# Start bytes of the tiles that TensorE reads, in a one-core hybrid decoder layer

## The chip, the core and the metric

The kernel runs on one core of one Trainium2 chip. The metric is the device time of one execution in microseconds (us). Three runs of the kernel before gave 320.55, 321.25 and 322.75 us, the median is 321.25 us. One further execution was profiled.

## What is computed

One pre-norm decoder layer over 256 tokens of width 1024, in float32, then a final RMSNorm:

```python
h = rms_norm(x, norm_g)
(qa, ka, va, ga, ub, vb, gb, qc, gc, ma, mb, mc) = split_cols(h @ w_in, IN_SPLITS)
out_a = moba_attention(rope(qa), rope(ka), va) * silu(ga)        # 6 heads of 128, causal
out_b = gmlp_spatial_gate(ub, vb, ln_g, w_spatial, b_spatial) * silu(gb)
out_c = memory_cross_attention(qc, rms_norm(mem, mem_norm_g), w_mem_kv) * silu(gc)
y = (sigmoid(ma) * (out_a @ w_branch_a) + sigmoid(mb) * (out_b @ w_branch_b)
     + sigmoid(mc) * (out_c @ w_branch_c))
x = rms_norm(x + y @ w_out, final_norm_g)
```

With 256 tokens there is one attention block, so branch A is plain causal attention. In branch B the spatial gate is `u * (tril(w_spatial) @ layer_norm(v) + b_spatial)`, with `b_spatial` added per token and group. Nearly all the work is the product of `h`, of the branch outputs and of `y` with weight matrices that are read once from HBM.

## The kernel before, in words

**Split operands.** Each float32 operand of the big products is cut into two parts of the type fp32r, a high and a low one. A product then takes three matmuls: high by high, high by low, low by high. The activations are cut once (`nh`/`nl`, `sh`/`sl`, `mh`/`ml`, `ah`/`al`, `obh`/`obl`, `och`/`ocl`, `yh`/`yl`). The weights are cut as they arrive: `split` (L250 to L270) lets ScalarE write `hi` (L260) and VectorE write `lo` as the weights minus `hi` (L264).

**Chunks.** The weights come in pieces of 128 partitions by 2048 floats. A piece is two chunks of 1024 columns each. `PLAN` and `chunks` (L189 to L202) give the order of all 136 chunks by hand. There are these kinds:

- `mvk` (L502, L508): keys and values of the memory tokens, the first eight chunks.
- `tok` (L481) and `fea` (L630): products of `n`. In `fea` the weights are the stationary operand, a chunk is eight matmuls of 512 columns with `hi` and eight of 256 columns with `lo`.
- `st` (L570): products of `n` and `s` with sums of weight blocks (a two by two scheme with seven products). Here `n` or `s` is stationary and `hi` or `lo` streams past it, six matmuls of 512 columns a chunk. The sums of weights are made by the DMA: a plain load into `form` (L233, SP queue), then an accumulating load on top of it (L236, GpSimd queue), and for some by VectorE (L240).
- `br` (L448 to L450 through `mm3`): the branch outputs `ah`/`al`, `obh`/`obl`, `och`/`ocl` are stationary, `hi` and `lo` stream. Twelve matmuls of 512 columns a chunk. Six `br` chunks take `ah` and `al`.
- `out` (the same lines): `y` with `w_out`, at the end; half of the second token tile in pieces of 256 columns.

**Buffers.** `hi` and `lo` are two tiles of five slots of 4096 bytes each (`SPL = 5`, L187). Chunk c uses slot c % 5, so it may be split when the matmuls of chunk c-5 have read that slot. `raw` has three buffers of 8192 bytes, `form0` and `form1` have 8192 bytes each.

**Order of the small work.** Attention, the spatial gate, softmax and the norms are units in a list. A planner, `Units` (L85 to L147), places them between the chunks by its own estimates of engine time and by due chunks. Loads are issued on the SP queue in program order, so a load waits behind the one ahead of it. `load` (L214) issues the pieces of plain weights, `load_wsp` (L698) the spatial weights with the spatial bias behind them in the same tile `wspb`, and `mix_gate` (L966) adds the bias to the mixed tokens and multiplies by `u`. Units decide the order of instructions while the program is built; nothing in it depends on run time.

**Where tiles begin.** Tiles are laid one behind another in each partition, in the order in which their tags first occur; a tile begins at a multiple of 32 bytes. In the built program before, the start bytes modulo 1024 are these:

| tile that TensorE reads | start byte modulo 1024 |
|---|---|
| `hi`, `lo` (weights, all five slots) | 736, 736 |
| `n`, `s`, `m`, `y` | 608 |
| `obh`, `obl`, `och`, `ocl` | 608 |
| `ah`, `al` | 736 |
| `cx`, `va`, `vb`, `wspb` | 608 |
| `qk` | 544 |

Inside a tile TensorE's operands begin at steps of 512 bytes (128 floats). So, modulo 512, the weights begin 128 bytes away from every activation except `ah` and `al`, which begin at the same byte. `raw` and `form0` begin at 736, `form1` at 608.

Of the kernel before, what the change touches and what calls it, by code (L numbers as in the profile page):

```python
# [24 lines left out]
F32 = mybir.dt.float32  # L25
# [3 lines left out]
OP = mybir.AluOpType  # L29
# [6 lines left out]
HA, GB, HC = 6, 6, 4  # L36
# [112 lines left out]


@with_exitstack
def tile_hybrid_layer(ctx: ExitStack, tc: tile.TileContext, mw, xT, mem, x, fin_g, ln_g, w, ws, w_sp, b_sp, rope, out):
    nc = tc.nc
    ctx.enter_context(tc.manual_schedule())
    const = ctx.enter_context(tc.tile_pool(name="const", bufs=1))
# [5 lines left out]
    V = {}  # L161

    def slot_tile(name, shape, tag, dt=F32):
        V[name] = act.tile(shape, dt, name=name, tag=tag)
        return V[name]
# [16 lines left out]
    def hsl(h):  # L182
        return slice(h * 128, (h + 1) * 128)


    LOPAD = 0
    RAW, SPL, LEAD, JT = 3, 5, 4, 2  # L187
    raw, hi, lo = {}, {}, {}
    chunks = []  # L189
# [17 lines left out]
    def raw_alloc(j):  # L207
        raw[j] = wts.tile([128, PIECE], F32, name="raw", tag="raw", bufs=RAW)

    def load_part(j, a, b):  # L210
        src = bass.AP(tensor=w.tensor, offset=w.offset + PLAIN.index(j) * 128 * PIECE + a, ap=[[PIECE, 128], [1, b - a]])
        nc.sync.dma_start(raw[j][:, a:b], src)

    def load(j):  # L214
        raw_alloc(j)
        parts = 2 if 18 <= j < 49 else 1
        for i in range(parts):
            load_part(j, i * PIECE // parts, (i + 1) * PIECE // parts)

# [30 lines left out]
    def split_alloc(c):  # L250
        if "hi" not in V:
            for n, pad in (("hi", 0), ("lo", LOPAD)):
                if pad:
# [442 lines left out]
        nc.sync.dma_start(V["lng"], rows(ln_g, BW))  # L696

    def load_wsp():  # L698
        t = slot_tile("wspb", [128, GB * 128 + 32], "trig")
        nc.sync.dma_start(t[:, 0:GB * 128 + GB], w_sp)  # L700
        V["wsp"], V["bst"] = t[:, 0:GB * 128].rearrange("p (g t) -> p g t", g=GB), t[:, GB * 128:GB * 128 + GB]

    def cut_wsp():
        for g in range(GB):
# [43 lines left out]
    U.add("consts", POOL, 1.3, setup_consts, after=["sx0"], wait=6.0)  # L748
    U.add("gmlp", None, 0, load_lng, after=["lns"], wait=8.0)
    U.add("wsp", None, 0, load_wsp, after=["rout2"], wait=8.0)  # L750
    U.add("cut", POOL, 1.6, cut_wsp, after=["wsp"])
    U.add("bsb", None, 0, load_bsb, after=["lna0", "lna1"], wait=8.0)
# [99 lines left out]
        return [] if n < 0 else [f"c{stage}{n}" if n < HC else f"a{stage}{n - HC}"]  # L852


    lst = const.tile([128, 2, 2], F32, name="lst")
    lrs = const.tile([128, 2], F32, name="lrs")

# [108 lines left out]
    def mix_gate(i, a):  # L966
        g = 2 * i + a
        pv, u = ST["mp", i][:, a * S:a * S + S].rearrange("p (t s) -> p t s", t=2), V["ut"][:, :, hsl(g)]
        nc.vector.scalar_tensor_tensor(u, pv, V["bst"][:, g:g + 1], u, op0=OP.add, op1=OP.mult)

    def turn_b(i):
        ST["bt", i] = p = bank()
# [48 lines left out]
    for i in range(2):  # L1021
        U.chain(f"mix{i}", (PE, 0.87, lambda i=i: mix_tok(i)), (DVE, 0.42, lambda i=i: mix_gate(i, 0)),
                (DVE, 0.42, lambda i=i: mix_gate(i, 1)), due=[at_br[0, 3] - 7 + i, at_br[0, 3] - 5 + i, at_br[0, 3] - 5 + i], after=["lna0", "lna1", "cut", "gts"])
# [125 lines left out]
    for c in range(n_br):  # L1149
        if chunks[c][0] == "st":  # L1150
            _, g, i, h = chunks[c]
# [6 lines left out]
    for c in range(n_br + 4):  # L1158
# [27 lines left out]
        if s % 2 == 1 and s // 2 in PLAIN:  # L1186
            q = PLAIN.index(s // 2) + 2
            if 4 < q < len(PLAIN):
                load(PLAIN[q])
            if q == 6:  # L1190
                load_mem()
# [132 lines left out]
```

## Time and profile before

| | value |
|---|---|
| runs | 320.55, 321.25, 322.75 us |
| profiled execution | 320.98 us |
| its span, from first to last instruction | 319.2 us |
| mean granted TensorE clock | 0.996 |
| matmuls | 1542 |
| first and last matmul, start | 0.84 us and 313.1 us |
| read from HBM | 73.02 MB |

The profile names an instruction by its line, its engine, its operation and its tiles, written `out<-in`. Matmuls overlap: a row's duration runs from the start of a matmul to its modelled end, so the time that a matmul takes from the stream is the distance between the start of it and the start of the next one. PEld is the loading of the stationary operand for the matmul to come, which runs while the one before streams. The chain of waits follows the last instruction back to what released it. In the windows view a number behind x counts the instructions that touch the window.

### The profile page before, as it was taken

How to read it: one execution, taken by the hardware profiler on the slowest of the kernel's cores; microseconds unless marked ns; L12 is line 12 of the kernel's file. 1: busy time of each engine (PE TensorE's matmuls, PEld its weight loads, DVE VectorE, ACT ScalarE, POOL GpSimd, SP SyncE). 2: the span in 40 equal slices, each digit the busy share in tenths (PEclk: the TensorE clock that was granted, in tenths of full speed). 3: DMA queues.
4: the chain of work that ended last, by engine and by line, in shares of the span. 5: the costliest groups of instructions: out<-in, count | busy, mean ns of one | idle time of the engine just before them, and what ended most of it. 6: DMA issues, size and time to landing. Idle time of an engine off the chain costs nothing.

```text
span 319.2 us, 4440 instructions
## 1 busy us (share of the span) xinstructions
PE 312.0 (98%) x1542; PEld 260.1 (81%) x1542; DVE 260.2 (81%) x376; ACT 227.8 (71%) x357; POOL 36.5 (11%) x55
## 2 busy tenths in 40 slices
PE   8999999999999999999999999999999999999992
PEld 4888888888888888888888888888888887888982
DVE  2878999996689887877599799998996599989432
ACT  3875989556997658877996968669758655576333
POOL 1000040030010013006003102004020031000022
PEclk9999999999999999999999999999999999999998
DMA  7999999789659879868967999778999789943003
GB/s 198 405 402 415 369 353 245 282 213 199 195 180 248 265 248 203 198 206 200 285 199 200 190 342 259 175 258 172 233 337 284 267 201 198 388 140 131 2 2 130
DMA packets 20470, 75.14 MB, mean 235 GB/s; under 512 B 2528, under 2 KB 3552, under 8 KB 18144
## 3 DMA queue, kind: packets, MB, share of 16 engines
q1 hardware_dynamic: 15984, 59.00, 52.3%
q0 software_dynamic: 4320, 15.73, 26.8%
q8 instruction: 12, 0.20, 0.2%
q10 hardware_dynamic: 144, 0.13, 0.1%
q14 instruction: 10, 0.08, 0.1%
HBM read 73.02 MB, written 1.05 MB: 232 GB/s over the span
## 4 chain that ended last, share of the span: by engine, by line
PE 77%; DMA 9%; DVE 6%; issue 4%; ACT 1%; POOL 0%; SPq 0%; ACTq 0%; POOLq 0%; DVEq 0%
PE acc L630 26%; PE acc L570 18%; DMA form<-in_ws_dram 7%; PE aux L502 3%; PE acc L508 3%; PE aux L570 3%; DVE lo L264 3%; PE acc L450 3%; PE acc L448 3%; PE acc L449 3%; PE aux L781 2%; DMA st<-in_mw_dram 2%; PE aux L481 2%; PE acc L481 2%; DVE form L240 1%
## 5 line engine op out<-in xcount | busy, mean ns | idle before, releaser
L264 DVE TENSOR_TENSOR lo<-form,hi 128x1024 fp32r<-128x1024 f32 x70 | 84.8, 1222 | 16.2 <-ACT hi L260 15.7
L260 ACT ACTIVATE hi<-form 128x1024 fp32r<-128x1024 f32 x70 | 73.4, 1057 | 23.3 <-DMA form<-in_ws_dram 8.6
L264 DVE TENSOR_TENSOR lo<-raw,hi 128x1024 fp32r<-128x1024 f32 x58 | 70.1, 1223 | 11.2 <-ACT hi L260 10.9
L260 ACT ACTIVATE hi<-raw 128x1024 fp32r<-128x1024 f32 x58 | 60.9, 1057 | 10.8 <-DMA raw<-in_w_dram 4.7
L630 PE MATMUL acc<-n,hi 128*128 128x512 f32 x240 | 61.0, 396 | 0.0
L236 POOL DMA_DIRECT2D form<-in_ws_dram x30 | 26.1, 871 | 232.9 <-DVE lo L264 84.6
L630 PEld LDWEIGHTS acc<-n,hi 128*128 128x128 f32 x240 | 43.9, 188 | 9.1
L570 PE MATMUL acc<-hi,s 128*128 128x512 f32 x96 | 33.1, 402 | 0.0
L630 PE MATMUL acc<-n,lo 128*128 128x256 f32 x240 | 32.5, 285 | 0.0
L630 PEld LDWEIGHTS acc<-n,lo 128*128 128x128 f32 x240 | 31.1, 188 | 1.5
L570 PE MATMUL acc<-hi,n 128*128 128x512 f32 x72 | 25.1, 404 | 0.0
L570 PEld LDWEIGHTS acc<-hi,s 128*128 128x128 f32 x96 | 18.1, 188 | 4.0
L570 PE MATMUL aux<-hi,s 128*128 128x512 f32 x64 | 21.1, 395 | 0.0
L570 PE MATMUL acc<-lo,s 128*128 128x512 f32 x48 | 18.9, 395 | 0.0
L570 PE MATMUL aux<-hi,n 128*128 128x512 f32 x48 | 16.1, 396 | 0.0
L570 PEld LDWEIGHTS acc<-hi,n 128*128 128x128 f32 x72 | 13.6, 188 | 2.9
L570 PEld LDWEIGHTS aux<-hi,s 128*128 128x128 f32 x64 | 12.1, 188 | 2.8
L570 PE MATMUL acc<-lo,n 128*128 128x512 f32 x36 | 14.2, 394 | 0.0
L570 PE MATMUL aux<-lo,s 128*128 128x512 f32 x32 | 12.7, 398 | 0.3 <-DVE lo L264 0.3
L643 ACT ACTIVATE qk<-acc 128x256 f32<-128x256 f32 x12 | 4.7, 390 | 11.7 <-PE acc L630 11.7
L240 DVE TENSOR_TENSOR form<-form,form 128x1024 f32<-128x1024 f32 x10 | 12.2, 1222 | 0.0
L570 PEld LDWEIGHTS aux<-hi,n 128*128 128x128 f32 x48 | 9.0, 188 | 2.1
(233 smaller groups left out, 581.8 us busy)
## 6 DMA issues: line engine op xcount, KB each, us to landing
raw<-in_w_dram SPq DMA_DIRECT2D x17, 1024.0 KB, 8.1
form<-in_ws_dram SPq DMA_DIRECT2D x30, 512.0 KB, 5.6
form<-in_ws_dram POOLq DMA_DIRECT2D x30, 512.0 KB, 8.5
raw<-in_w_dram SPq DMA_DIRECT2D x24, 512.0 KB, 7.3
st<-in_mw_dram SPq DMA_DIRECT2D x7, 384.0 KB, 7.5
raw<-in_w_dram SPq DMA_DIRECT2D x8, 256.0 KB, 7.2
xk<-in_x_dram SPq DMA_DIRECT2D x2, 512.0 KB, 7.5
xt<-in_xT_dram SPq DMA_DIRECT2D x2, 512.0 KB, 9.6
```

The source lines that it names most:

```text
L236: nc.gpsimd.dma_start(form_half(i, h), block(g, b, h), accum_op=OP.add)
L240: nc.vector.tensor_tensor(form_half(i, h), form_half(i, h), form_half(1 - i, h), OP.add)
L260: nc.scalar.activation(hi[c][:, a:b], raw[c // 2][:, o + a:o + b], AF.Copy)
L264: nc.vector.tensor_tensor(lo[c][:, a:b], raw[c // 2][:, o + a:o + b], hi[c][:, a:b].bitcast(F32), OP.subtract)
L448: nc.tensor.matmul(p, s_hi, m_hi, start=first, stop=False)
L449: nc.tensor.matmul(p, s_hi, m_lo, start=False, stop=False)
L450: nc.tensor.matmul(p, s_lo, m_hi, start=False, stop=last)
L481: nc.tensor.matmul(acc[name, o][t], src[:, k0 + i, tsl(t)], wt[c][:, i * 512:(i + 1) * 512], start=c == 8 and i + j == 0, stop=c == 11 and ...
L502: nc.tensor.matmul(acc["mv", 0][t][:, a:b], src[:, k, tsl(t)], wt[:, a:b], start=k + n == 0, stop=k == KD - 1 and n == len(parts) - 1)
L508: nc.tensor.matmul(p, wt, m, start=k == 0 and j < HC, stop=k == KD - 1 and j >= HC)
L570: nc.tensor.matmul(p, x[:, k0 + k, tsl(t)], wt[c][:, a * 512:(a + 1) * 512], start=first and a + j == 0, stop=half == 1 and a + j == 3, sk ...
L630: nc.tensor.matmul(o, wt, m, start=i == 0, stop=i == len(passes) - 1, skip_group_check=True)
```

## The change

Five edits:

1. The spatial bias gets a tile of its own, `b_col`, in the pool `const`. That pool grows by 32 bytes, and all tiles behind it move by that.
2. `wspb`, of 3200 bytes, becomes `wsp`, of 3072 bytes. Tiles behind it no longer stand 128 bytes further modulo 1024.
3. `LOPAD` goes from 0 to 64 floats: an unused tile of 256 bytes stands between `hi` and `lo`.
4. The spatial bias is loaded by a DMA of its own, 6 floats a partition, right behind that of the spatial weights on the SP queue. `mix_gate` takes it from `b_col`.
5. `load` cuts one piece of weights less into two DMAs (the bound 49 becomes 47).

Start bytes modulo 1024 in the built program, before and with the change:

| tile | before | with the change |
|---|---|---|
| `hi` | 736 | 640 |
| `lo` | 736 | 896 |
| `n`, `s`, `m`, `y`, `obh`, `obl`, `och`, `ocl` | 608 | 640 |
| `ah`, `al` | 736 | 640 |
| `cx`, `va`, `vb`, `wsp` | 608 | 640 |
| `qk` | 544 | 576 |
| `raw`, `form0`, `form1` | 736, 736, 608 | 640, 896, 640 |

```diff
-    LOPAD = 0
+    LOPAD = 64
...
-        parts = 2 if 18 <= j < 49 else 1
+        parts = 2 if 18 <= j < 47 else 1
...
     def load_wsp():
-        t = slot_tile("wspb", [128, GB * 128 + 32], "trig")
-        nc.sync.dma_start(t[:, 0:GB * 128 + GB], w_sp)
-        V["wsp"], V["bst"] = t[:, 0:GB * 128].rearrange("p (g t) -> p g t", g=GB), t[:, GB * 128:GB * 128 + GB]
+        slot_tile("wsp", [128, GB, 128], "trig")
+        nc.sync.dma_start(V["wsp"], w_sp)
+        nc.sync.dma_start(b_col, b_spt)
...
+    b_col = const.tile([128, GB], F32, name="b_col")
...
-        nc.vector.scalar_tensor_tensor(u, pv, V["bst"][:, g:g + 1], u, op0=OP.add, op1=OP.mult)
+        nc.vector.scalar_tensor_tensor(u, pv, b_col[:, g:g + 1], u, op0=OP.add, op1=OP.mult)
```

The host gives the bias as an array of its own, `b_spt`, no longer behind the spatial weights.

No engine's instructions change their order. Only the SP queue has other rows. Around the spatial weights it holds this before:

```order
L233 DMA form_401<-in_ws_dram 128x1024
L769 DMA qk<-mid 32x256 x4
L700 DMA wspb<-in_w_sp_dram 128x774
L233 DMA form_401<-in_ws_dram 128x1024
L212 DMA raw<-in_w_dram 128x1024 x2
```

and this with the change:

```order
L233 DMA form_403<-in_ws_dram 128x1024
L769 DMA qk<-mid 32x256 x4
L700 DMA wsp<-in_w_sp_dram 128x768
L701 DMA b_col<-in_b_spt_dram 128x6
L233 DMA form_403<-in_ws_dram 128x1024
L212 DMA raw<-in_w_dram 128x1024 x2
```

One small DMA stands ahead of the next `form` load. Further down, one piece of weights (that of the second `br` piece) comes as one DMA; here is the piece of the difference on the SP queue:

```order
 L212 DMA raw<-in_w_dram 128x1024 x2
-L233 DMA form_326<-in_ws_dram 128x1024 x2
-L212 DMA raw<-in_w_dram 128x1024 x2
-L233 DMA form_326<-in_ws_dram 128x1024 x2
+L233 DMA form_328<-in_ws_dram 128x1024 x2
+L212 DMA raw<-in_w_dram 128x2048
+L233 DMA form_328<-in_ws_dram 128x1024 x2
 L212 DMA raw<-in_w_dram 128x2048 x2
```

Two loads of 512 KB have become one of 1024 KB; the names of `form` differ only in a buffer number.

More of the change, by code (lines that the diff above doesn't have):

```diff
@@ L151, in tile_hybrid_layer @@
 @with_exitstack
-def tile_hybrid_layer(ctx: ExitStack, tc: tile.TileContext, mw, xT, mem, x, fin_g, ln_g, w, ws, w_sp, b_sp, rope, out):
+def tile_hybrid_layer(ctx: ExitStack, tc: tile.TileContext, mw, xT, mem, x, fin_g, ln_g, w, ws, w_sp, b_sp, b_spt, rope, out):
     nc = tc.nc
@@ L1307 @@
         "ws": np.ascontiguousarray(ws),
-        "w_sp": np.concatenate([np.asarray(w_spatial)[0].transpose(2, 0, 1).reshape(128, -1),
-                                np.asarray(b_spatial)[0].T], axis=1),
+        "w_sp": np.ascontiguousarray(np.asarray(w_spatial)[0].transpose(2, 0, 1)),
         "b_sp": np.ascontiguousarray(np.asarray(b_spatial)[0]),
+        "b_spt": np.ascontiguousarray(np.asarray(b_spatial)[0].T),
         "rope": np.ascontiguousarray(rope),
```

## The prediction

> **What bounds the kernel now.** I read three views in this order: busy shares, the chain of waits in order of time, and then TensorE's own rows, because the first two leave only TensorE. The page's first two parts:
>
> ```profile
> PE 312.0 (98%) x1542; PEld 260.1 (81%) x1542; DVE 260.2 (81%) x376; ACT 227.8 (71%) x357; POOL 36.5 (11%) x55
> PE   8999999999999999999999999999999999999992
> ```
>
> TensorE has work in nearly every slice. So a change counts if it makes the stream of matmuls denser, or if it makes a wait that the stream does not have. The chain of waits shows where the stream itself sets the time (start, length in us, what):
>
> ```profile
> 39.84 5.62 PE acc L630 x32
> 45.46 2.79 PE acc L570 x12
> ...
> 202.15 5.63 PE acc L630 x32
> 207.81 0.39 ACT jt L643
> ...
> 238.10 12.28 DMA form<-in_ws_dram
> 250.49 1.07 ACT hi L260
> ...
> 263.92 1.23 DVE lo L264
> 265.19 1.43 PE aux L570 x5
> ...
> 272.20 2.79 PE aux L570 x12
> ...
> 313.93 0.30 ACT rt L1134
> ```
>
> Until 207.8 us and again from 265.2 us to the last matmul the chain is TensorE. In between it runs through loads, ScalarE and VectorE, because one wait at 265 us is traced back there:
>
> ```profile
> PE aux L570 <- DVE lo L264: 0.3, 1, 0.3
> ```
>
> That is the only wait of TensorE for data after the start that the table of waits shows, 0.3 us. So this second chain is as long as TensorE's own work there, within half a microsecond. It has no room to follow a faster TensorE.
>
> **What a matmul takes.** The front gives the start bytes. Only `ah` and `al` begin at the same byte modulo 1024 as the weights; the others begin 128 bytes off. The timeline of TensorE holds both cases next to each other (start, length to the modelled end):
>
> ```profile
> 213.18 0.39 PE L448 MATMUL acc<-hi,ah 128*128 128x512 f32 x1
> 213.41 0.39 PE L449 MATMUL acc<-lo,ah 128*128 128x512 f32 x1
> ...
> 218.63 0.40 PE L570 MATMUL aux<-hi,s 128*128 128x512 f32 x1
> 218.87 0.40 PE L570 MATMUL aux<-lo,s 128*128 128x512 f32 x1
> 219.11 0.62 PE L570 MATMUL aux<-hi,s 128*128 128x512 f32 x2
> ...
> 224.22 0.39 PE L448 MATMUL acc<-hi,ah 128*128 128x512 f32 x1
> ```
>
> ```profile
> 243.54 0.39 PE L448 MATMUL acc<-hi,obh 128*128 128x512 f32 x1
> ...
> 249.11 0.40 PE L570 MATMUL aux<-hi,n 128*128 128x512 f32 x1
> ```
>
> From 213.18 to 218.63 two `br` chunks run, 24 matmuls with `ah` and `al`: 5.45 us, 227.1 ns each. From 218.63 to 224.22 four `st` chunks run, 24 matmuls of 512 columns as well: 5.59 us, 232.9 ns each. From 243.54 to 249.11 the same code lines as in the first case run with `obh` and `obl`: 5.57 us, 232.1 ns. Same line, shape and accumulators, other start bytes: 5.0 ns, or 2%. The `fea` chunks agree with the slow case: 5.62 us for 16 matmuls of 512 columns and 16 of 256; at 232 ns the first take 3.71 us, which leaves 119 ns for one of 256 columns.
>
> That it is the start bytes is my reading of these rows, not shown. What else differs between `ah` and `obh` is only which tile they are. The Trainium skill speaks against it: "SBUF — State Buffer", section "Who interferes with whom", says that TensorE never waits on anyone at the memory, and "TensorE: Matmul & The Clock Gate", section "Part 2: What happens when you issue a matmul", says that its two read ports are independent and loading the next weights takes nothing from the running matmul. By that rule the start byte costs nothing and the sum would be zero; the 5.0 ns between the two rows above do not fit it.
>
> **The change, part by part.** First the counts. Matmuls that read `hi` or `lo`, all of the run, and those that must be taken off:
>
> ```profile
> 0.00:313.40 313.40, 238.57 (x826) 152.91 (x826) 164.71 (x144) 142.94 (x145) 1.00 0.81 238
> ```
>
> ```profile
> 0.00:313.40 313.40, 141.25 (x548) 88.06 (x548) 164.71 (x144) 1.00 0.81 238
> ```
>
> ```profile
> L630 PE MATMUL acc<-n,lo 128*128 128x256 f32 x240 | 32.5, 285 | 0.0
> L448 PE MATMUL acc<-hi,ah 128*128 128x512 f32 x24 | 9.4, 390 | 0.0
> L450 PE MATMUL acc<-hi,al 128*128 128x512 f32 x24 | 9.4, 390 | 0.0
> L449 PE MATMUL acc<-lo,ah 128*128 128x512 f32 x24 | 9.3, 389 | 0.0
> L508 PE MATMUL acc<-m,lo 128*128 128x256 f32 x32 | 5.0, 282 | 0.0
> L448 PE MATMUL aux<-hi,y 128*128 128x256 f32 x16 | 4.5, 283 | 0.0
> L449 PE MATMUL aux<-lo,y 128*128 128x256 f32 x16 | 4.5, 283 | 0.0
> L450 PE MATMUL aux<-hi,y 128*128 128x256 f32 x16 | 4.5, 282 | 0.0
> L502 PE MATMUL aux<-hi,m 128*128 128x256 f32 x4 | 1.2, 449 | 0.0
> ```
>
> With `hi`: 826, less 48 that have `ah` or `al` and 36 of 256 columns, leaves 742 of 512 columns that stand 128 bytes off now and begin at the same byte afterwards. With `lo`: 548, less 24 with `ah` and 288 of 256 columns, leaves 236 of 512 columns that go from 128 bytes off to 256 bytes off. The 24 with `ah` go from the same byte to 256 bytes off.
>
> - **hi at the same byte:** 742 x 5.0 ns = 3.71 us less.
> - **lo 256 bytes off:** no row has this distance. A bound on one side is the same byte, 5.0 ns less; on the other the distance of 128, nothing. In steps of 512, in which the operands stand, 256 is a distance of its own, as far from the fast case as it can be, but also twice the slow one. I take the middle, 2.5 ns: 236 x 2.5 = 0.59 us less, and 24 x 2.5 = 0.06 us more for those with `ah`.
> - **The 288 narrow matmuls with `lo`:** half as long, so at most half the effect, 2.5 ns either way, 0.72 us. I take zero.
> - **Given back between 230 and 265 us.** The second chain starts from TensorE through the buffers (ScalarE waits for `acc` of a `br` chunk at 229.9 us) and then has its own length: load, accumulating load, splits.
>
> ```profile
> 229.88 1.06 ACT L260 ACTIVATE hi<-form 128x1024 fp32r<-128x1024 f32 x1 [1.66 <-PE acc L450]
> 250.49 1.06 ACT L260 ACTIVATE hi<-form 128x1024 fp32r<-128x1024 f32 x1 [3.58 <-DMA form<-in_ws_dram]
> ```
>
> ```profile
> 230.00:265.20 35.20, 34.86 (x152) 1.00 0.91 274
> ```
>
> What TensorE gains in this stretch it waits for at 265 us. Of its 152 matmuls 24 have `ah` or `al`, 8 of them with `lo`; of the other 128, two thirds (85) stream `hi`, 43 `lo`. Lost again: 85 x 5.0 + 43 x 2.5 - 8 x 2.5 = 0.51 us.
> - **VectorE's split:** it reads `form` or `raw` and `hi`, and writes `lo`, now 256 bytes further than `hi`. The row below holds `form0` (same byte as `hi`) and `form1` (128 off), and its durations lie within 27 ns around 1222. I take zero.
>
> ```profile
> L264 DVE TENSOR_TENSOR lo<-form,hi x70: 1203/1222/1230, 41.5 to 276.3; 128x1024 fp32r<-128x1024 f32 x70
> ```
>
> - **The small bias DMA and the merged load:**
>
> ```profile
> 144.52 0.58 SPq L700 DMA_DIRECT2D wspb<-in_w_sp_dram  x1
> ...
> 190.90 0.90 SPq L212 DMA_DIRECT2D raw<-in_w_dram  x2
> ```
>
> ```profile
> 193.66 1.66 DVE L969 SCALAR_TENSOR_TENSOR ut<-aux,wspb,ut 128x256 f32<-128x256 f32 x4
> ```
>
> ```profile
> 220.00 1.04 ACT L260 ACTIVATE hi<-raw 128x1024 fp32r<-128x1024 f32 x1
> ```
>
> The bias DMA needs one more issue on SP, some 0.6 us like the row of the spatial weights, and the `form` load and the piece of plain weights that follow on that queue wait for it. Its reader, `mix_gate`, runs at 193.7 us, 49 us later. The loads behind it feed splits that TensorE does not wait for: its table of waits above has nothing but the one at 265 us. The price, if that cover were gone, is the same 0.6 us. The merged load is issued at 190.9 us, and the first half of its piece is split at 220.0 us. Both count nothing.
>
> Sum: 3.71 + 0.59 - 0.06 - 0.51 = 3.73 us. The profiled execution took 320.98 us (span 319.2), so 317.25 us. The median of the three runs is 0.27 us above the profiled one, so I say **317.4 us**. By the bounds of `lo` and of the narrow matmuls the likeliest case reaches from 316.1 (`lo` as fast as `hi`, narrow ones gain) to 318.7 us (`lo` gains nothing, narrow ones lose).
>
> **Rivals.**
>
> - *The start bytes do nothing* (the rule above): `ah` is faster for a reason of its own. For it: no row varies the start byte alone. Against it: the rows from 213 to 224 us, where the pace changes with the tile from one matmul to the next and not with the stretch of time. Time: 321.0 us.
> - *lo's offset costs what hi gains.* If 256 off is worse than 128 off, up to the longest distance in the rows (218.63 to 218.87 to 219.11, 240 ns), then 236 x 8 + 24 x 13 + 288 x 4 ns = 3.35 us come back; of 3.71 less the 0.43 us that `hi` loses at 265 us nothing is left, 321.0 us. For it: only that no row excludes it.
> - *Slower: the same byte is the bad case.* TensorE streams one operand while it loads the next weights; if the two streams meet because they begin at the same byte, and `ah` escapes it, each of the 742 matmuls goes to 240 ns: 742 x 8 = 5.9 us more, 326.9 us. It decides from 4.3 ns a matmul on (3.2 us over 742). Against it: the `ah` rows are the very case, and are fast.
>
> **How the numbers follow.** A measurement of this kernel can tell about 1% from no change, here 3.2 us, so faster means below 318.0 us. The forecast has 0.62, most of it (0.54) below 318.0; no effect 0.18; `lo` takes it back 0.12; slower 0.08. That gives 0.55 faster, 0.37 within 1%, 0.08 slower. The range, 315.2 to 321.0 us, takes in the forecast's bounds, somewhat more below since `lo` could also pass the fast row, and the two cases without a gain.
>
> **What would show it.** In the profile after, `fea` rows of 32 matmuls take 5.54 us where they took 5.62, the modelled durations of `hi` with `obh` fall to the 390 ns of `ah`, and the rows of `hi` with `ah` stay. The distances of `lo` matmuls tell the open term. The wait at 265 us grows from 0.3 to about 0.8 us, or the next one stands elsewhere in 250 to 265 us. I am wrong if matmuls with `hi` and `obh` still take 232 ns, or if they are faster and waits for VectorE or DMA fill what they leave.

## The result and the profile after

The change makes the kernel faster by 1.4%. Four executions of it took 316.41 to 317.53 us, median 316.94 us; four of the kernel before took 320.55 to 322.75 us, median 321.48 us. The ratio is 0.986, interval [0.982, 0.990]. A second measurement of the same kernel, with other executions of both, gave 0.990, interval [0.986, 0.993] (317.21 against 321.22 us, `e8_change_again` below). One execution of `e1_bias_dma_old_bytes` (388.62 us) and one of `e2_lo_same_byte` (321.99 us) ran slow; the ratios below leave them out, the medians of 320.30 and 318.1 us do not. The prediction was 317.4 us. The profiled execution took 316.41 us, its span is 314.7 us where it was 319.2 us.

The page's first two parts, TensorE's rows:

```profile
PE 307.0 (98%) x1542; PEld 259.1 (82%) x1542; DVE 259.8 (83%) x376; ACT 228.2 (73%) x357; POOL 36.4 (12%) x55
PE   7999999999999999999999999999999999999992
```

TensorE is busy 5.0 us less and still 98% of the span; VectorE and ScalarE do the same work as before. So the stream of matmuls got denser, and little idle time came in its place: the span is 4.5 us shorter. The chain of waits of the changed kernel (start, length in us, what), at the places that the prediction showed:

```profile
39.38 5.57 PE acc L630 x32
44.95 2.72 PE acc L570 x12
...
199.88 5.57 PE acc L630 x32
...
235.83 10.84 DMA form<-in_ws_dram
...
260.21 1.23 DVE lo L264
261.44 0.04 issue
261.49 1.45 PE aux L570 x5
```

A group of 32 `fea` matmuls takes 5.57 us (5.62 before), twelve of `st` 2.72 us (2.79 before). The second chain is still there, from the loads through VectorE to TensorE; its accumulating load took 10.84 us in this execution, 12.28 us in the one before. The timeline of TensorE (start, length to the modelled end), the same stretch of the program as in the prediction:

```profile
210.73 0.39 PE L448 MATMUL acc<-hi,ah 128*128 128x512 f32 x1
210.95 0.39 PE L449 MATMUL acc<-lo,ah 128*128 128x512 f32 x1
...
216.17 0.39 PE L570 MATMUL aux<-hi,s 128*128 128x512 f32 x1
216.39 0.39 PE L570 MATMUL aux<-lo,s 128*128 128x512 f32 x1
...
221.61 0.39 PE L448 MATMUL acc<-hi,ah 128*128 128x512 f32 x1
...
240.65 0.39 PE L448 MATMUL acc<-hi,obh 128*128 128x512 f32 x1
...
246.09 0.39 PE L570 MATMUL aux<-hi,n 128*128 128x512 f32 x1
```

From 210.73 to 216.17 run 24 matmuls with `ah` and `al`, from 216.17 to 221.61 the 24 of `st`, from 240.65 to 246.09 the 24 with `obh` and `obl`. Each stretch takes 5.44 us, 226.7 ns a matmul. Before, the three took 5.45, 5.59 and 5.57 us: the first is as it was, the others have come down to it. The groups of TensorE by line (count, busy us, mean ns to the modelled end) say the same, 389 and 390 ns where `ah` had 390 all along:

```profile
L570 PE MATMUL aux<-hi,s 128*128 128x512 f32 x64 | 20.7, 389 | 0.0
L450 PE MATMUL acc<-hi,obl 128*128 128x512 f32 x24 | 9.3, 390 | 0.0
```

Before, these two had 395 and 394 ns:

```profile
L570 PE MATMUL aux<-hi,s 128*128 128x512 f32 x64 | 21.1, 395 | 0.0
L450 PE MATMUL acc<-hi,obl 128*128 128x512 f32 x24 | 9.5, 394 | 0.0
```

The table of what TensorE waits for:

```profile
PE aux L354 <- PEq L1314: 0.8, 1, 0.8
PE acc L508 <- ACT hi L422: 0.8, 1, 0.8
```

Both rows belong to the start; the second one is not in the table of the kernel before. The wait for `lo` (0.3 us before) is not in the table; the chain above still ends in it, and in the timeline the `lo` matmul that starts at 261.49 stands 0.21 us further from its neighbour than a matmul takes (0.51 us before). The small parts of the change, on the SP queue and on VectorE:

```profile
143.05 0.58 SPq L700 DMA_DIRECT2D wsp<-in_w_sp_dram  x1
143.68 0.43 SPq L701 DMA_DIRECT2D b_col<-in_b_spt_dram  x1
144.21 0.36 SPq L233 DMA_DIRECT2D form<-in_ws_dram  x1
```

```profile
L264 DVE TENSOR_TENSOR lo<-form,hi x70: 1205/1221/1228, 40.6 to 272.8; 128x1024 fp32r<-128x1024 f32 x70
```

The bias DMA delays the `form` load behind it by some 0.5 us, and the split's median is 1221 ns (1222 before).

### The profile page after: what moved, and what is told of

The parts are those of the page before. It is cut to its first block, busy times and chain, and to the rows that moved or that the text cites. A ratio compares the mean times of both kernels' runs of the same rounds, so it can differ in the third digit from the quotient of the medians.

```text
span 314.7 us, 4438 instructions
## 1 busy us (share of the span) xinstructions
PE 307.0 (98%) x1542; PEld 259.1 (82%) x1542; DVE 259.8 (83%) x376; ACT 228.2 (73%) x357; POOL 36.4 (12%) x55
## 4 chain that ended last, share of the span: by engine, by line
PE 82%; DMA 7%; DVE 4%; issue 3%; ACT 2%; POOL 0%; ACTq 0%; SPq 0%; POOLq 0%; DVEq 0%
PE acc L630 27%; PE acc L570 18%; DMA form<-in_ws_dram 6%; PE aux L570 5%; PE acc L508 4%; PE acc L450 3%; PE acc L448 3%; PE acc L449 3%; PE aux L502 3%; DVE lo L264 2%; PE aux L781 2%; PE acc L481 2%; PE aux L481 2%; DMA raw<-in_w_dram 2%; PE aux L449 1%
## 5 line engine op out<-in xcount | busy, mean ns | idle before, releaser
L264 DVE TENSOR_TENSOR lo<-form,hi 128x1024 fp32r<-128x1024 f32 x70 | 84.8, 1221 | 15.4 <-ACT hi L260 14.8
L264 DVE TENSOR_TENSOR lo<-raw,hi 128x1024 fp32r<-128x1024 f32 x58 | 70.1, 1222 | 10.2 <-ACT hi L260 10.0
L630 PE MATMUL acc<-n,hi 128*128 128x512 f32 x240 | 60.2, 393 | 0.0
```

What stands on the lines that cost most here:

```text
L264: nc.vector.tensor_tensor(lo[c][:, a:b], raw[c // 2][:, o + a:o + b], hi[c][:, a:b].bitcast(F32), OP.subtract)
L630: nc.tensor.matmul(o, wt, m, start=i == 0, stop=i == len(passes) - 1, skip_group_check=True)
```

## The experiments

My theory: the distance between the start bytes of the two operands of a matmul sets its time, and what TensorE gains near 260 us it waits for, since the second chain has a length of its own. The rivals: another part of the change did it (the bias DMA, the merged load); the absolute place in memory counts, not the distance; the wait near 260 us is VectorE's own work. In all tables "distance" is the start byte of `hi` or `lo` less that of the activation. Times of one matmul that stand without a profile row are medians of the distance from its start to the next start in the trace.

**The small edits alone.** Edits 4 and 5 stay; `LOPAD` and the bytes of `wspb` go back, so all distances are the old ones.

```diff
-    LOPAD = 64
+    LOPAD = 0
...
-        slot_tile("wsp", [128, GB, 128], "trig")
+        t = slot_tile("wspb", [128, GB * 128 + 32], "trig")
+        V["wsp"] = t[:, 0:GB * 128].rearrange("p (g t) -> p g t", g=GB)
```

> The bias tile, its DMA and the merged load are in, but the spatial weights keep a tile of 3200 bytes and nothing stands between hi and lo, so the weights again begin 128 bytes from the activations (hi and lo at 768, activations at 640, ah and al at 768). Theory (the distance of the start bytes makes the time): no gain, 321 us like the kernel before, 232 ns for a matmul of 512 columns, 227 ns with ah and al. Rival (the other edits gave part of the gain): the part that is theirs stays, under 320 us, up to 317 if it is all theirs.

320.30 us, ratio 1.000 [0.997, 1.003]. In its timeline of TensorE the stretches with `ah` and with `s` differ as before the change, 5.48 and 5.59 us:

```profile
213.04 0.40 PE L448 MATMUL acc<-hi,ah 128*128 128x512 f32 x1
...
218.52 0.40 PE L570 MATMUL aux<-hi,s 128*128 128x512 f32 x1
...
224.11 0.39 PE L448 MATMUL acc<-hi,ah 128*128 128x512 f32 x1
```

So the bias DMA and the merged load are worth nothing that can be measured, and the whole effect lies in the bytes.

**Only the weights moved away again.** The changed kernel with 128 unused bytes ahead of `hi`. `hi` stands 128 bytes off every activation and `lo` 384, this time from `ah` and `al` too.

```diff
-    LOPAD = 64
+    HIPAD, LOPAD = 32, 64
...
-            for n, pad in (("hi", 0), ("lo", LOPAD)):
+            for n, pad in (("hi", HIPAD), ("lo", LOPAD)):
```

> The changed kernel with 128 bytes more ahead of hi: hi is 128 bytes from all activations, lo 384 bytes; ah and al too, which had the same byte in both kernels. Theory: all matmuls of 512 columns go to 232 ns, those with ah and al as well (227 before), so 321 to 321.5 us. Rival (ah is fast for another reason, or the gain came from where the activations stand and not from the distance): ah stays at 227 ns, or the time stays near 317 us.

320.93 us, ratio 1.000 [0.999, 1.002]: the gain is gone. The timeline of TensorE and its groups:

```profile
213.20 0.40 PE L448 MATMUL acc<-hi,ah 128*128 128x512 f32 x1
...
218.80 0.40 PE L570 MATMUL aux<-hi,s 128*128 128x512 f32 x1
...
224.40 0.40 PE L448 MATMUL acc<-hi,ah 128*128 128x512 f32 x1
```

```profile
L448 PE MATMUL acc<-hi,ah 128*128 128x512 f32 x24 | 9.5, 395 | 0.0
L449 PE MATMUL acc<-lo,ah 128*128 128x512 f32 x24 | 9.5, 395 | 0.0
```

The stretch with `ah` now takes 5.60 us, 233.3 ns a matmul, and its rows show 395 ns where the kernel before and the changed one had 389 or 390. Nothing about the tile, the line or the accumulator is different. This is the run that turns my reading of the rows into something shown: moving only the weights' start makes the same instruction slower, and it also makes `ah`, the tile that had been fast, slow.

**All tiles 128 bytes on.** An unused tile ahead of everything: weights and activations at byte 768, `lo` at 0, distances as in the change.

```diff
     b_col = const.tile([128, GB], F32, name="b_col")
+    const.tile([128, 32], F32, name="allpad")
```

> The changed kernel with an unused tile of 128 bytes ahead of all tiles that TensorE reads: the weights and the activations begin at byte 768, lo at 0, so every distance between them is that of the change and only the absolute byte differs. My theory (the distance between the operands counts): 226 to 227 ns a matmul of 512 columns, 316.4 to 317.7 us. Rival (byte 640 itself is a good place, or 608 and 736 bad ones): another pace, if 232 ns then 321 us.

316.53 us (one execution; 320.43 us for the kernel before beside it). Its timeline:

```profile
210.28 0.39 PE L448 MATMUL acc<-hi,ah 128*128 128x512 f32 x1
...
215.72 0.39 PE L570 MATMUL aux<-hi,s 128*128 128x512 f32 x1
...
221.16 0.39 PE L448 MATMUL acc<-hi,ah 128*128 128x512 f32 x1
```

5.44 us for each stretch. Distance counts; whether the tiles begin at 640 or at 768 does not, as far as one execution shows.

**The pad between `hi` and `lo`.** Twice, on different occasions, the changed kernel without the pad, so that `lo` begins at the same byte as all others:

```diff
-    LOPAD = 64
+    LOPAD = 0
```

> The change without the 256 bytes between hi and lo: all at 640. Theory (a distance of 256 bytes is as good as none for the matmuls, and VectorE does not care): 317 us like the changed kernel, matmuls that stream lo at 226 to 227 ns as there. Rival (the 256 bytes are needed, because VectorE writes lo while it reads hi and raw, or because lo and hi must differ for TensorE): over 318 us, with VectorE's split over 1230 ns or lo matmuls over 230 ns.

> The changed kernel without the 256 bytes between hi and lo once more, on the same chip as the changed kernel. Theory: the same as the changed kernel within the intervals, 317 us. Rival (the 256 bytes help): about 318 us again, 1 us or more slower, with the long wait near 261 us in the profile again.

beside the change itself once more, with no edit:

> The changed kernel once more, beside the one without the 256 bytes. Theory (nothing but the distance modulo 256 counts): the two are the same within their intervals, 317 us each, and what differs between single runs is the wait of TensorE for VectorE near 261 us. Rival (the 256 bytes help): this one 1 us or more faster than the other, intervals apart.

Without the pad the ratios are 0.991 [0.988, 0.994] and 0.990 [0.987, 0.993]; with it 0.990 [0.986, 0.993]. After the first eight chunks all medians of 512 columns are 226 to 227.5 ns in the three kernels, `lo` as well as `hi`. So 256 bytes off is the same as no distance, and the pad does nothing. The first comparison (318.1 against 316.9 us) had looked like a gain of the pad; side by side on one chip, 317.55 and 317.21 us, it is not there.

**Other distances.** One execution each, `HIPAD, LOPAD = 8, 8` (distances 32 and 64) and `24, 24` (96 and 192).

> The changed kernel with hi 32 and lo 64 bytes from the activations. Theory A (a matmul slows as soon as the distance is no multiple of 256 bytes): both 232 ns, about 321 us. Theory B (it is a matter of how far in 256 bytes): values between 227 and 232 ns, hi nearer to 227; 317 to 320 us. Theory C (only the half, 128, is bad): both 227, about 317 us.

> The changed kernel with hi 96 and lo 192 bytes from the activations, beside the run with 32 and 64 (there wide matmuls took 229 to 234 ns at both, narrow ones with lo at 64 bytes 114 ns). Theory A (for wide matmuls every distance that is no multiple of 256 bytes costs): 229 to 235 ns for hi and lo, about 320 us. Theory B (the cost grows with the distance up to 128 bytes): hi at 96 near 233 ns, lo at 192, 64 bytes below 256, near 230. The narrow ones at 192: 114 ns if the sign of the distance does not matter, 119 to 120 if it does.

319.58 and 320.50 us, nearer to the 320.93 us of 128 bytes than to the change. The timelines of TensorE, the first `st` matmuls of the stretch and the first matmul behind it, first with distances of 32 and 64:

```profile
217.86 0.39 PE L570 MATMUL aux<-hi,s 128*128 128x512 f32 x1
218.09 0.39 PE L570 MATMUL aux<-lo,s 128*128 128x512 f32 x1
218.32 0.63 PE L570 MATMUL aux<-hi,s 128*128 128x512 f32 x2
218.78 0.40 PE L570 MATMUL aux<-lo,s 128*128 128x512 f32 x1
...
223.41 0.39 PE L448 MATMUL acc<-hi,ah 128*128 128x512 f32 x1
```

then with 96 and 192:

```profile
218.43 0.40 PE L570 MATMUL aux<-hi,s 128*128 128x512 f32 x1
218.67 0.39 PE L570 MATMUL aux<-lo,s 128*128 128x512 f32 x1
218.89 0.63 PE L570 MATMUL aux<-hi,s 128*128 128x512 f32 x2
219.36 0.39 PE L570 MATMUL aux<-lo,s 128*128 128x512 f32 x1
...
223.98 0.40 PE L448 MATMUL acc<-hi,ah 128*128 128x512 f32 x1
```

The stretch of 24 takes 5.55 us in both, 231.1 ns a matmul, and so do the stretches with `ah` and with `obh` in both traces: less than the 232.1 to 233.3 ns of 128 and 384 bytes, more than the 226.7 ns of the change. Inside the stretch the steps differ: in the second kernel the step from a `hi` to the next start is 0.23 to 0.24 us and from a `lo` 0.22 to 0.23. By medians over the trace, one for each line and pair of tiles, without the first eight chunks:

| distance | 512 columns, ns | 256 columns (`fea`), ns |
|---|---|---|
| 0 and 256 | 226 to 227.5 | 120 |
| 32 | 229 to 235.5 | |
| 64 | 229 to 232 | 114 |
| 96 | 232 to 236 | |
| 128 and 384 | 229 to 238 | 119 |
| 192 | 225 to 227 in `st` and `br`, 230 to 235 in `tok`, 227 to 231 in `out` | 118 |

These medians do not give each distance its own price, because a step also depends on its neighbours: in `e1_bias_dma_old_bytes`, where `hi` and `lo` in `tok` stand at the same distance of 128 throughout, the medians are 229 ns for one accumulator and 237 for the other. The 225 to 227 ns at 192 bytes stand beside 232 to 236 ns of `hi` at 96, and the stretch as a whole is as long as with 32 and 64. So that 192 bytes are as good as none is not shown; a run with `lo` alone at 192 would be needed. Nor are the 114 ns a gain: the `hi` matmuls between them take 234 ns, and 32 `fea` matmuls of that kernel take 5.56 us by its chain of waits, as long as in the change (5.57):

```profile
39.85 5.56 PE acc L630 x32
```

**The `fea` low parts 64 bytes further** than in the change, alone, to see whether the 114 ns can be had without moving `hi`:

```diff
-                V[n] = wts.tile([128, SPL, CH], F32R, name=n, tag=n)
-        hi[c], lo[c] = V["hi"][:, c % SPL, :], V["lo"][:, c % SPL, :]
+                V[n] = wts.tile([128, SPL, CH + pad], F32R, name=n, tag=n)
+        o = 16 if chunks[c][0] == "fea" else 0
+        hi[c], lo[c] = V["hi"][:, c % SPL, :], V["lo"][:, c % SPL, o:o + CH]
```

> The changed kernel, but lo is written 64 bytes further inside its slot in the fea chunks alone (slots 256 bytes longer), so that the 240 narrow matmuls of 256 columns get the distance of 64 bytes and all wide ones keep a multiple of 256. Theory (the distance acts on each matmul by itself): narrow ones 114 ns, 240 x 5.5 = 1.3 us less than the changed kernel, all before 207 us, so about 315.6 us, less what the wait at 261 us takes back. Rival (the 114 ns came from hi at 32 bytes or from the whole layout): narrow ones stay at 120 ns, 317 us.

316.65 us, ratio 0.988 [0.984, 0.991], no different from the change. The narrow matmuls take 118 ns, not 114, and a group of 32 5.54 us:

```profile
39.43 5.54 PE acc L631 x32
```

15 groups of 32 at 0.03 us would be 0.45 us; the wait near 261 us was 0.80 us in this execution, and what was won lies inside it.

**The give-back.** Collected from the traces: when the second accumulating load of the chain landed, when VectorE started the `lo` for which TensorE waits (chunk 117 of the 136), and by how much TensorE's step there was longer than a matmul.

| kernel | landed, us | `lo` starts, us | between, us | wait, us |
|---|---|---|---|---|
| before | 250.38 | 263.92 | 13.54 | 0.51 |
| e1 (old distances) | 249.58 | 263.12 | 13.54 | none |
| e3 (128) | 249.39 | 262.92 | 13.53 | none |
| the change | 246.67 | 260.21 | 13.54 | 0.21 |
| e6 | 246.81 | 260.35 | 13.54 | 0.80 |
| e7 | 246.81 | 260.35 | 13.54 | 0.80 |
| e8 (the change again) | 247.32 | 260.85 | 13.53 | 1.07 |
| e2 | 248.22 | 261.76 | 13.54 | 1.31 |
| e9 | 248.22 | 261.76 | 13.54 | 1.28 |

The wait is counted from start to start; the step behind it is some 0.11 us longer than a matmul as well, in all kernels that wait, and the column leaves that out. `e2_lo_same_byte` and `e9_lo_same_again` have a second wait of 0.2 us near 250 us. The time between is the same to 0.01 us in all of them: once the load has landed, ScalarE and then VectorE work without a break until that `lo`, whatever TensorE does. The timelines of `e8_change_again`, VectorE's and then TensorE's, show the two ends:

```profile
248.52 1.22 DVE L264 TENSOR_TENSOR lo<-form,hi 128x1024 fp32r<-128x1024 f32 x1 [3.39 <-ACT hi L260]
...
260.85 1.22 DVE L264 TENSOR_TENSOR lo<-form,hi 128x1024 fp32r<-128x1024 f32 x1
```

```profile
260.60 0.61 PE L570 MATMUL aux<-hi,s 128*128 128x512 f32 x2
262.12 0.50 PE L570 MATMUL aux<-lo,s 128*128 128x512 f32 x1 [0.91 <-DVE lo L264]
```

VectorE sat idle for 3.39 us up to 248.52 us, when the landed load had been made into `hi`, and TensorE stands 0.91 us at 262.12 us (from the modelled end of the matmul before; from start to start it is the 1.07 us of the table). If the load is the cause, an earlier landing must take the wait away. On the SP queue the load of the final norm's scale (`fing`, 512 KB, read only at the end) stands between the `form` loads and a 1 MB load of weights, and transfers beside the accumulating loads. Three kernels move it behind them, the first in the changed kernel, the second with the 64 bytes of `e7_fea_lo64`, the third in the kernel before:

```diff
-    U.add("fin", None, 0, load_fin, after=[f"c{at_br[1, 2]}"], wait=8.0)
+    U.add("fin", None, 0, load_fin, after=[f"c{at_br[1, 2] + 8}"], wait=8.0)
```

> The changed kernel; the load of the final norm's scale (fing, 512 KB written, read only at the end of the kernel) moves on the SP queue from 235 us, between the form loads of the second chain, to behind the loads for that chain, some 12 us later. Nothing else moves. My theory (what TensorE gains is given back near 261 us because the second accumulating form load lands at 247 us, after which VectorE works without a break until the split that TensorE waits for): 512 KB at the 274 GB/s of that stretch is 1.9 us, so that load lands up to 1.9 us sooner and the wait near 261 us (0.2, 1.1, 1.3, 1.3, 0.8 us in the kernels at 227 ns so far) is gone: 316.3 to 316.9 us, 0.3 to 1 us under the change. Rival (VectorE's own work between 250 and 261 us sets it, or the load is late for its own reasons): the wait stays at 0.5 to 1.3 us and the time at 317.2.

> As e10_fing_later, and the low parts of the fea chunks stand another 64 bytes on, as in e7_fea_lo64, where the narrow matmuls with lo took 118 instead of 120 ns and the wait near 261 us took it back. My theory: with that wait gone the 0.5 us comes through, 315.8 to 316.4 us, 0.8 to 1.5 us under the change. Rival (the wait stays, or the 118 ns was nothing): 316.7 to 317.2 us.

> The kernel before with the same move of the fing load alone. My theory (TensorE at 232 ns waits little there, 0.3 us in its profile): at most 0.5 us less, 320.6 to 321.2 us, and no wait near 265 us. Rival (the load's move is worth as much without the change): 1 us or more less, 320.2 us or below.

| kernel | us | ratio | landed, us | wait, us |
|---|---|---|---|---|
| e10 | 315.99 | 0.986 [0.984, 0.989] | 244.73 | none |
| e12 | 315.54 | 0.985 [0.982, 0.987] | 246.74 | 0.86 |
| e13 (kernel before) | 320.33 | 0.999 [0.997, 1.002] | 246.94 | none |

In `e10_fing_later` the load landed 1.9 us or more before any kernel of the table above, and its timelines, VectorE's and then TensorE's, have no wait for that `lo`:

```profile
245.92 1.22 DVE L264 TENSOR_TENSOR lo<-form,hi 128x1024 fp32r<-128x1024 f32 x1 [0.69 <-ACT hi L260]
...
258.70 1.22 DVE L264 TENSOR_TENSOR lo<-form,hi 128x1024 fp32r<-128x1024 f32 x1
```

```profile
260.70 0.61 PE L570 MATMUL aux<-hi,s 128*128 128x512 f32 x2
261.16 0.39 PE L570 MATMUL aux<-lo,s 128*128 128x512 f32 x1
```

The two steps from 260.70 to 261.16 are 0.23 us each. That `lo` starts 13.97 us after the landing here and 14.83 us in `e13_before_fing_later`, no longer 13.54: in these two the load does not set its start any more. In `e13_before_fing_later`, at the old pace, the same move changes nothing that can be measured. One expectation was wrong: I wrote that nothing else moves, but the 1 MB load that had stood behind `fing` was issued 4 us sooner too (231.26 instead of 235.34 us), so the earlier landing is owed to both. And `e12_fing_later_fea_lo64` missed: in its profiled execution the load landed at 246.74 us in spite of the move, and TensorE waited 0.86 us. That execution took 316.41 us, its three others 315.34 to 315.54, which fits a wait that comes and goes with the landing of the load; they have no trace, so that is argued and not shown. All three times lie below the ranges expected for them, but the kernel before took 320.43 us beside them, 0.8 us less than beside `e8_change_again`; the ratios are what can be compared. The intervals of e8, e10 and e12 overlap. `e12_fing_later_fea_lo64` has the lowest median of all, but that it beats the change is not shown.

## Why the prediction was right, point by point

**The bound** was read rightly. The chain is TensorE outside the stretch from 230 to 265 us, denser matmuls shorten it, and the second chain ends in the same `lo`.

**The start bytes** are the cause, as `e3_weights_128` and `e1_bias_dma_old_bytes` show from both sides. The rival that they do nothing falls with that, and so does the slower one, that the same byte is the bad case: it is the fast one in every kernel. The Trainium skill's "SBUF — State Buffer", section "Who interferes with whom", gives TensorE two read ports, for the streaming operand and for the weights, independent and shared with no other engine; from that no start byte would matter. Here the same `ah` matmuls took 226.7 ns and, with only the weights 128 bytes further, 233.3 ns. The measurement decides. What in the memory or in TensorE's reading makes the difference is not shown by any run.

**The sum was right because two of its terms were off by about the same amount.** To see the terms without the wait, I compare `e13_before_fing_later` with `e10_fing_later`: neither waits near 260 us, and only the bytes and the small edits lie between them. From the first matmul's start to the last one's it is 311.55 against 307.23 us, 4.32 us less; the prediction had 4.24 us before the give-back (3.71 + 0.59 - 0.06). Of the 4.32 us, 0.22 lie in the first eight chunks, where TensorE waits for splits and where the table of waits of e13 has one wait more (0.3 us); behind them it is 4.10 us. Summed from start to start in the two traces:

| term | predicted gain, us | measured, us |
|---|---|---|
| `hi`, 742 wide | 3.71 | 174.72 - 171.55 = 3.17 |
| `lo`, 236 wide | 0.59 | 55.87 - 54.64 = 1.23 |
| with `ah`, `al` (72) | -0.06 | 16.39 - 16.32 = 0.07 |
| `lo`, 288 narrow | 0 | 35.12 - 35.23 = -0.11 |

- *`hi`* was put too high. The 5.0 ns came from stretches of `br` and `st` chunks and were carried over to the 240 in `fea`. There a group of 32 fell from 5.62 to 5.57 us, not to the 5.54 us that I had named as the sign: 0.05 us over 16 matmuls, some 3 ns. The mean over all 742 is 3.17 us / 742 = 4.3 ns. From start to start, without the first eight chunks, it is 5.0 ns for the 440 outside `fea`, as read, and 3.6 ns for the 240 in `fea`. Why `fea` gains less is not shown.
- *`lo`* was put too low. I took the middle between the fast case and none, 2.5 ns; measured are 1.23 us / 236 = 5.2 ns, and 5.0 ns for the 220 behind the first eight chunks, as much as `hi` outside `fea`. The step that failed is "a distance of its own": 256 bytes is no distance, it repeats the fast case. The reading of 512 as the period had no row behind it. The rival that `lo` takes back what `hi` gains falls too.
- *The narrow ones and `ah`* gain and lose nothing worth counting, as said.

**The give-back** was of the right kind and about the right size, but the sign that I had named for it, a wait that grows, did not show in the profile of the change. I had 0.5 us more, a wait of 0.8 us where the table of waits had 0.3; counted from start to start as in the table above, that is 1.0 us where it was 0.5. In the six kernels at the new pace with the `fing` load in its old place it was 0.21, 0.80, 0.80, 1.07, 1.28 and 1.31 us. At the old pace it was not always there either: 0.51 us in the profile of the kernel before, none in e1 and e3. The profiled execution of the change had the lowest of the six: its load landed 0.14 us before that of `e6_all_128`, and TensorE came to that place 0.45 us later, having waited 0.8 us at the start. What I had not seen is how far the landing of one load moves the wait between two executions of one kernel: 246.67 us with a wait of 0.21 us in the profile of the change, 247.32 us with 1.07 us in `e8_change_again`.

**The costs put at nothing** were nothing: the split on VectorE (1222 and 1221 ns), the bias DMA and the merged load (ratio 1.000 in `e1_bias_dma_old_bytes`).

So of 4.1 to 4.3 us that the matmuls gain, about one can be lost again near 261 us. The two measurements of the change, 4.5 and 4.0 us under the kernel before, have intervals from 3.3 to 5.9 us and from 2.1 to 4.5 us: whole times cannot tell how much was given back, only the traces can. They also cannot tell my 317.4 us from 317.52 us, which is what 317.25 us and the 0.27 us between the profiled execution and the median add up to.

## What to carry to other kernels

When one tile's matmuls run faster than others of the same shape and line, compare start bytes before anything else, and prove it by shifting one operand alone: a pad of a few floats is a one-line experiment. A gain of 2% on each matmul comes through only as far as the loads and splits that feed TensorE have slack, so look for a second chain of nearly equal length and measure its fixed length over several executions. Where a term has no row, test the assumption that sets its scale (here the period of the distance); two errors of half a microsecond cancelled here, and need not elsewhere.

## What the runs showed of the hardware that I had not expected

- For fp32r matmuls of 512 columns, a distance of 0 or 256 bytes between the start of the weights and that of the activations gives 226 to 227.5 ns by medians, 128 or 384 bytes 229 to 238 ns, at granted clocks of 0.994 to 0.998.
- With `hi` and `lo` 32 and 64 bytes off, and with 96 and 192, a stretch of 24 such matmuls took 5.55 us, between the 5.44 us of 0 and 256 bytes and the 5.57 to 5.60 us of 128 and 384. Whether 64 bytes ahead and 64 behind cost the same is open.
- In alternating streams a step of one kind can hide in the next: with `hi` 32 and `lo` 64 bytes off, narrow matmuls took 114 instead of 120 ns and the wide ones between them 234 instead of 227, and the sum stayed (5.56 and 5.57 us for 32). So the price of a distance is read from whole stretches, not from single steps.
- One accumulating load of 512 KB took 10.8 to 12.3 us from issue to landing at the same place of the program, and 8.9 to 10.8 us where `fing` was not beside it, while the 13.54 us of ScalarE's and VectorE's work behind it varied by 0.01 us in the nine kernels of the table.
